# Transposing the q and k stacks of three attention branches on TensorE instead of by DMA

## The chip, the cores and the metric

The kernel runs on one core of a Trainium2 chip. The metric is the device time of one execution in microseconds (us). The engines are TensorE (PE in the profile, with PEld for its weight loads), VectorE (DVE), ScalarE (ACT), GpSimd (POOL) and SyncE (SP), which here only issues DMAs. Each engine takes its instructions from a queue of its own, in order. On-chip data lies in SBUF, the results of matmuls in PSUM; GpSimd does not read PSUM here.

## What is computed

One layer of a hybrid decoder over a sequence of 2048 positions with 1024 channels: an RMS norm, one input projection, three token mixers side by side, a SiLU gate on each, one output projection and the residual. Cut to what matters here:

```python
h = rms_norm(x, norm_g)
proj = einsum('bsd,de->bse', h, w_in)
# A) forgetting attention, 8 heads of 64: logits q.k/8 + c[t] - c[s], causal softmax, times v
fq = rms_norm(heads(fq), q_norm_g); fk = rms_norm(heads(fk), k_norm_g)
fox = forgetting_attention(fq, fk, fv, log_f) * silu(fg)
# B) trailing means over 2/4/8/16 positions, a linear map for each group
pool = multiscale_pool(px, w_pool, pool_scale) * silu(pg)
# C) stick-breaking attention, 4 heads of 64: sigmoids with running products, strictly causal
sb = stick_breaking_attention(sq, sk, sv) * silu(sg)
out = x + einsum('bse,ed->bsd', concat([fox, pool, sb]), w_out)
```

## The kernel before

The sequence is cut into 16 blocks of 128 positions and runs backwards. A value that needs more than 16-bit precision is carried as a pair of f16 numbers, a high part and a low part (`pairs16`, L339: ScalarE casts the high part, VectorE subtracts it from the source to get the low part). So a projection is three f16 matmuls for each of 8 slices of the 1024 channels (`project`, L315).

The work comes in five phases: `a` and `b` (four forgetting heads each, class `Fox`), `s` (four stick-breaking heads, class `Stick`, with the pooling branch `p` woven in) and `o` (the output projection). In `a`, `b` and `s` each of the 16 blocks does the following.

- Project q, k, v and the gate into PSUM (`proj`, tiles `pqk` and `pvg`). In `a` and `b`, `stages` (L704) then normalises q and k through ScalarE, VectorE and GpSimd into the SBUF tile `qn`; in `s`, q and k are taken straight from PSUM.
- `stacks` (L455) builds the f16 pairs of q and k in the tile `st` (high and low part of k, high and low part of q, each of 4 heads and 64 channels wide) and issues one DMA transpose on SP's queue into `qT` (L464). A function `place` is put off by `SCD` = 5 steps: on VectorE it copies the transposed k into the key cache `Kc` (L467), and then, by two copies of 64 partitions each, writes q's low and high parts in swapped order over the place where k stood (L469). After that the first half of `qT` holds q with its parts swapped, the second half q in order.
- `qk` computes the scores of a head in one or two chunks of at most 1024 columns. `scores` (L396) takes one of the two PSUM tiles with the tag `sp` and does two matmuls for each 512 columns (L404), one with each half of `qT`, so that all four products of the parts come together. In `a` and `b` VectorE adds the forget bias and takes the maximum (L736), and ScalarE does the exponentials (L746). In `s` ScalarE does sigmoids (L875), GpSimd masks them (L877, L878), and VectorE scans the products (L883).
- `split_t` (L416) makes an f16 pair of each chunk in a buffer `pp` (ScalarE or VectorE casts, L430 and L432; GpSimd subtracts, L433) and transposes it by DMA from SP's queue (L435). The `pp` buffers are a ring of `PB` = 5, which the rows of x also use (`transpose_rows`, L371) before their DMA transpose.
- `pv` multiplies by v, three heads later (`DEPTH` = 3, L1202). In `s`, `steps` (L814) also makes differences of v on PE (L821) from a pair that has just been cast.

What sets the order: `projections` (L1120) is a generator that yields after every slice of a projection, that is after three matmuls; `advance` (L1190) pulls it and calls `tick` at each step, which runs what `later` put off. The main loop (L1218) lays the heads of block k between the steps by a written list of due steps (`LEADS`, L76). This gives the program order. The order in each engine's queue is then made from it at compile time by the framework's scheduler (L1309), which takes program order as priority and its own model for durations.

Of the kernel before, what the change touches and what calls it, by code (L numbers as in the profile page):

```python
# [10 lines left out]
F16 = mybir.dt.float16  # L11
BF16 = mybir.dt.bfloat16
AF = mybir.ActivationFunctionType
ALU = mybir.AluOpType
# [4 lines left out]
P = 128  # L19
KT = 8  # L20
D = 1024
HD = 64
NH = 4
# [13 lines left out]
GR4 = 0  # L37
GR2 = 1
QSB = 2
SWE = 'vv'  # L40
KCE = 'v'
SCD = 5
M5 = 2
FE = 's'
OMS = 'g'
# [17 lines left out]
LEAD = 10  # L63
DEPTH = 3
TB = 4
PB = 5
FHIA = 'sv'
FHIB = 'ssv'
FLO = 'gg'
# [56 lines left out]
def hybrid(ctx: ExitStack, tc, xN, w_in, w_pT, w_out, ng, b_f, qg, kg, w_pool, p_scale, bands, out):  # L126
    nc = tc.nc
    v, s, g, t, sy = nc.vector, nc.scalar, nc.gpsimd, nc.tensor, nc.sync
# [4 lines left out]
    const = ctx.enter_context(tc.tile_pool(name="const", bufs=1))  # L133
# [3 lines left out]
    at = ctx.enter_context(tc.tile_pool(name="at", bufs=2))  # L137
    sm = ctx.enter_context(tc.tile_pool(name="sm", bufs=3))
    pj = ctx.enter_context(tc.tile_pool(name="pj", bufs=PJ, space=PSUM))
    ps = ctx.enter_context(tc.tile_pool(name="ps", bufs=2, space=PSUM))  # L140
# [5 lines left out]
    def pick(pattern, k):  # L146
        return {"v": v, "g": g, "s": s}[pattern[k % len(pattern)]]
# [6 lines left out]
    def later(k, fn):  # L154

        if k:
            waiting.append([k, fn])
        else:
            fn()
# [19 lines left out]
    ident = const.tile([P, P], F32, name="ident")  # L179
# [4 lines left out]
    g.affine_select(tri, ones, [[-1, P]], ALU.is_ge, 0.0, base=0, channel_multiplier=1)  # L184
    id16 = const.tile([P, P], BF16, name="id16")
    g.tensor_copy(id16, ident)
    zero = at.tile([P, P], BF16, name="zero", tag="oa")
    g.memset(zero, 0.0)
    cmask = const.tile([P, P], BF16, name="cmask")
# [37 lines left out]
    class Weights:  # L227
# [12 lines left out]
        def measure(self, kt):  # L240
            for a, n in enumerate(self.widths):
                wr = self.raw(kt, a, "wm")
                junk = at.tile([P, n], BF16, name=f"jk{self.name}_{kt}_{a}", tag="pp", bufs=PB)
                acc = self.fa[:, a * KT + kt:a * KT + kt + 1]
# [53 lines left out]
        def weigh(self, kt, eng):  # L298
            held = self.held[:, kt]
            junk = at.tile([P, self.widths[0]], BF16, name=f"jh_{kt}", tag="L", bufs=LB) if eng is s else at.tile([P, self.widths[0]], BF16, name=f"jh_{kt}", tag="pp", bufs=PB)  # L300
            acc = self.fa[:, kt:kt + 1]
# [37 lines left out]
    def pairs16(hi, lo, src, scale, eng=v):  # L339

        s.activation(hi, src, AF.Copy, scale=scale)
        eng.scalar_tensor_tensor(lo, src, scale, hi, ALU.mult, ALU.subtract)  # L342
# [6 lines left out]
    def squares(j, xn):  # L349
        junk = at.tile([P, D], BF16, name=f"xj{j}", tag="pp", bufs=PB)  # L350
        ssq = sm.tile([P, 1], F32, name=f"ssq{j}", tag="ssq")
        s.activation(junk, xn, AF.Square, accum_out=ssq)
        return ssq
# [17 lines left out]
    def transpose_rows(src, scale, tag, park=None):  # L371
        pp = at.tile([P, 2 * D], F16, name=f"pp{tag}", tag="pp", bufs=PB)
        pairs16(pp[:, 0:D], pp[:, D:2 * D], src, scale[:, 0:1], pick(XLO, park or 0))
        x = xp.tile([P, 2, KT, P], F16, name=f"xT{tag}", tag="xT", bufs=XB)
        sy.dma_start_transpose(x.rearrange("p a k t -> p (a k) t"), pp)
        if park is not None:
            keep_x(park, x)
        return x
# [37 lines left out]
    def split_t(p32, n, tag, h, all_, hi_eng, lo_eng):  # L416
# [3 lines left out]
        if k == 0:  # L420
            shared["pp"] = at.tile([P, 2 * CH], F16, name=f"pp{tag}", tag="pp", bufs=PB)
            shared["tt"] = at.tile([P, 2 * CH // P, P], F16, name=f"tt{tag}", tag="tt", bufs=TB)
# [27 lines left out]
    def heads(ap):  # L450
        return ap.rearrange("p (h d) -> p h d", h=NH)
# [2 lines left out]

    def stacks(tag, j, qsrc, ksrc, sc, Kc):  # L455

        st = at.tile([P, 2, NH, P], F16, name=f"st{tag}", tag="qs", bufs=QSB)
        pairs16(st[:, 0, :, 0:HD], st[:, 0, :, HD:P], heads(ksrc), sc)
        pairs16(st[:, 1, :, 0:HD], st[:, 1, :, HD:P], heads(qsrc), sc)
        qT = at.tile([P, 2 * NH, P], F16, name=f"qT{tag}", tag="qT", bufs=QTB)  # L460
        if j % 4 == 3:
            Kc[j // 4] = big.tile([P, NH, 512], F16, name=f"K{tag}", tag="K", bufs=KB)
        o_ = (j % 4) * P
        sy.dma_start_transpose(qT, st.rearrange("p a h d -> p (a h d)"))  # L464

        def place():
            pick(KCE, 0).tensor_copy(Kc[j // 4][:, :, o_:o_ + P], qT[:, 0:NH])  # L467
            for k in range(2):
                pick(SWE, k).tensor_copy(qT[k * HD:k * HD + HD, 0:NH], qT[HD - k * HD:P - k * HD, NH:2 * NH])  # L469
            placed.add(tag)  # L470

        later(SCD, place)
        return qT
# [839 lines left out]
```

## Time and profile before

| | us |
|---|---|
| median of 3 runs | 1418.04 |
| lowest and highest run | 1412.04, 1418.87 |
| profiled execution, its own time | 1417.73 |
| its span, first to last instruction | 1415.7 |

| engine | busy, us | share of the span | instructions |
|---|---|---|---|
| PE | 1209.6 | 85% | 9068 |
| DVE | 997.1 | 70% | 2093 |
| ACT | 702.0 | 50% | 1356 |
| POOL | 634.1 | 45% | 615 |

All of these come from one profiled execution. A matmul's busy time includes its way through the array, which overlaps with the next matmul, so a busy PE is not a PE at its peak. [...] "L467" is line 467 of the kernel. Where a row says that an engine waited for something, the engine's queue had nothing else to run in that time: the waiting instruction was at its head.

### The profile page before, as it was taken

The numbers are of one execution on the slowest core, as the hardware profiler recorded it, in microseconds if no ns is written. First come the engines' busy times: TensorE is split into PE (matmuls) and PEld (weight loads), VectorE is DVE, ScalarE is ACT, GpSimd is POOL, SyncE is SP. The second block draws the span as 40 slices with busy tenths as digits, with TensorE's granted clock in tenths as the row PEclk, the third lists the DMA queues.
The fourth block names the chain that finished last, engine by engine and source line by source line (L and its number), as shares of the span: only waits on it lengthen the run. The fifth ranks groups of instructions, "written<-read, shape, count | busy, mean of one in ns | idle before, by whom it ended". The sixth has DMA issues, their size and how long they took to land.

```text
span 1415.7 us, 24981 instructions
## 1 busy us (share of the span) xinstructions
PE 1209.6 (85%) x9068; PEld 642.2 (45%) x9068; DVE 997.1 (70%) x2093; ACT 702.0 (50%) x1356; POOL 634.1 (45%) x615
## 2 busy tenths in 40 slices
PE   7788879787887889897987888978988997779998
PEld 3344445444444445454544544444544553444443
DVE  5777889889998567786888655556574669865731
ACT  6555546555554446664667644545455564432210
POOL 0133345445455234553656654555455464623300
PEclk9889899999998989999999999999999999989999
DMA  6689999998999999996999998687886888999853
GB/s 215 176 169 203 214 188 221 200 196 182 210 210 209 210 227 207 202 177 135 184 217 191 227 207 186 146 158 161 173 175 142 172 196 226 225 277 287 225 160 89
DMA packets 617068, 275.25 MB, mean 194 GB/s; under 512 B 552561, under 2 KB 590833, under 8 KB 616945
## 3 DMA queue, kind: packets, MB, share of 16 engines
q1 hardware_dynamic: 605600, 239.93, 80.4%
q10 hardware_dynamic: 10832, 33.67, 7.9%
q8 instruction: 71, 1.16, 0.4%
q14 instruction: 53, 0.43, 0.1%
q0 software_dynamic: 512, 0.07, 0.0%
HBM read 102.60 MB, written 34.67 MB: 97 GB/s over the span
## 4 chain that ended last, share of the span: by engine, by line
PE 18%; DVE 11%; issue 9%; DMA 8%; POOL 8%; ACT 5%; SPq 1%; POOLq 0%; ACTq 0%; DVEq 0%
PE pr L319 11%; DVE rrs L883 5%; POOL pps L433 5%; DMA qTs<-sts 2%; DMA qTb<-stb 2%; PE pqks L319 2%; DVE Lb L736 2%; DMA xTm<-ppm 1%; ACT pps L430 1%; ACT Lb L746 1%; POOL rrs L877 1%; PE sps L404 1%; DMA ttb<-ppb 1%; PE pp L319 1%; POOL ppb L433 1%
## 5 line engine op out<-in xcount | busy, mean ns | idle before, releaser
L433 POOL TENSOR_TENSOR ppb<-Lb,ppb 128x1024 f16<-128x1024 f32 (+7 forms) x96 | 151.6, 1593 | 150.3 <-ACT ppb L430 68.9
L433 POOL TENSOR_TENSOR ppa<-La,ppa 128x1024 f16<-128x1024 f32 (+7 forms) x96 | 152.7, 1604 | 141.9 <-DVE ppa L432 53.4
L433 POOL TENSOR_TENSOR pps<-rrs,pps 128x640 f16<-128x640 f32 (+7 forms) x96 | 171.3, 1790 | 75.2 <-ACT pps L430 74.8
L319 PE MATMUL pr<-wo,xTm 128*128 128x512 f16 x768 | 172.2, 386 | 8.1 <-DMA xTm<-ppm 5.3
L883 DVE TENSOR_TENSOR_SCAN rrs<-rrs 128x640 f32<-128x640 f32 (+7 forms) x64 | 109.5, 1714 | 68.3 <-POOL rrs L877 43.8
L430 ACT CAST pps<-rrs 128x640 f16<-128x640 f32 (+7 forms) x96 | 76.1, 796 | 142.0 <-DVE rrs L883 127.3
L746 ACT ACTIVATE Lb<-Lb,nmb 128x640 f32<-128x640 f32 (+7 forms) x96 | 85.6, 892 | 80.3 <-DVE nmb L740 75.4
L746 ACT ACTIVATE La<-La,nma 128x640 f32<-128x640 f32 (+7 forms) x96 | 85.5, 891 | 77.0 <-DVE nma L740 53.5
L319 PEld LDWEIGHTS <-xTm 128*128 128x128 f16 x768 | 75.8, 99 | 100.9 <-issue 8.8
L319 PEld LDWEIGHTS <-xTb 128*128 128x128 f16 x768 | 77.0, 103 | 92.6 <-issue 16.7
L404 PE MATMUL spa<-Ka,qTa 128*128 128x512 f16 (+3 forms) x320 | 83.7, 371 | 36.8 <-DVE mma L736 35.2
L319 PEld LDWEIGHTS <-xTs 128*128 128x128 f16 x768 | 74.4, 99 | 86.9 <-issue 3.3
L319 PEld LDWEIGHTS <-xTx 128*128 128x128 f16 x720 | 72.6, 105 | 89.3 <-issue 25.5
L319 PE MATMUL pqkb<-wb,xTb 128*128 128x512 f16 x384 | 101.7, 408 | 0.3 <-ACT wb L277 0.3
L404 PE MATMUL spb<-Kb,qTb 128*128 128x512 f16 (+3 forms) x320 | 79.7, 361 | 23.4 <-DVE mmb L736 20.7
L319 PE MATMUL pp<-auxp,xTp 128*128 128x512 f16 x384 | 96.9, 404 | 0.0
L319 PE MATMUL pqka<-wa,xTx 128*128 128x512 f16 x336 | 95.3, 434 | 1.3 <-DVE cr L562 1.3
L319 PE MATMUL pvgb<-wb,xTb 128*128 128x512 f16 x384 | 96.1, 390 | 0.0
L875 ACT ACTIVATE rrs<-sps,nc 128x640 f32<-128x640 f32 (+7 forms) x96 | 80.5, 863 | 30.3 <-PE sps L404 28.8
L319 PE MATMUL pqks<-ws,xTs 128*128 128x512 f16 x384 | 92.1, 385 | 0.7 <-DVE vo L342 0.4
L404 PE MATMUL sps<-Ks,qTs 128*128 128x512 f16 (+3 forms) x320 | 73.2, 361 | 21.2 <-DVE qTs L469 16.6
L319 PE MATMUL pvgs<-ws,xTs 128*128 128x512 f16 x384 | 90.9, 379 | 0.0
(307 smaller groups left out, 2804.4 us busy)
## 6 DMA issues: line engine op xcount, KB each, us to landing
xn<-in_xN_dram SPq DMA_DIRECT2D x16, 512.0 KB, 5.5
xTd<-xTx ACTq DMA_DIRECT2D x16, 512.0 KB, 4.3
xTb<-xTd ACTq DMA_DIRECT2D x16, 512.0 KB, 4.6
xTs<-xTd ACTq DMA_DIRECT2D x16, 512.0 KB, 4.3
xTp<-xTd ACTq DMA_DIRECT2D x16, 512.0 KB, 4.3
go<-gat SPq DMA_DIRECT2D x16, 512.0 KB, 7.6
mt<-mix SPq DMA_DIRECT2D x16, 512.0 KB, 5.6
xr<-in_xN_dram SPq DMA_DIRECT2D x16, 512.0 KB, 4.4
```

What stands on the lines that cost most here:

```text
L319: t.matmul(psum, x[:, xa, kt, :], wt[:, wa, c0:c0 + n], start=(kt == 0 and i == 0), stop=(kt == KT - 1 and i == 2))
L404: t.matmul(sp[:, b - c0 + off:e - c0 + off], qT[:, a * NH + h, :], Kc[b // 512][:, h, b % 512:b % 512 + e - b], start=(a == 0), stop=(a == ...
L430: s.copy(hi, p32)
L433: lo_eng.tensor_tensor(lo, p32, hi, ALU.subtract)
L736: v.tensor_tensor_reduce(lt, sp, negc[:, h, c0:c1_], c1[:, 0:1], 4 * NEG if a == 0 else mm[:, a - 1:a], ALU.add, ALU.max, mm[:, a:a + 1])
L746: s.activation(ls[a], ls[a], AF.Exp, bias=nm[:, 0:1], accum_out=la[:, a, h:h + 1])
L875: s.activation(gg, sp, AF.Sigmoid, scale=self.nc2[:, 0:1])
L877: g.affine_select(gg[:, 0:P], gg[:, 0:P], [[1, P]], ALU.is_gt, 1.0, base=0, channel_multiplier=-1)
L883: v.tensor_tensor_scan(gg, gg, gg, init, ALU.mult, ALU.bypass)
```

## The change

The stack gets a third plane, so that q's high part and q's low part each stand twice, side by side, in planes of their own. The DMA transpose goes. `place` takes a score tile (`sp`) from PSUM, transposes the 4 blocks of k and the 8 of q on PE with an f16 identity, and copies the results by ScalarE straight into the key cache and into `qT`. With q's parts written twice, the two matmuls of a score are k with the doubled high part and k with the doubled low part; the four products are the same as before. `place` comes 2 steps after the stack instead of 5. The ring of part buffers has 4 buffers instead of 5.

```diff
-SWE = 'vv'
-KCE = 'v'
-SCD = 5
+SCD = 2
...
-PB = 5
+PB = 4
...
+    idh = const.tile([P, P], F16, name="idh")
+    g.tensor_copy(idh, ident)
...
     def stacks(tag, j, qsrc, ksrc, sc, Kc):
 
-        st = at.tile([P, 2, NH, P], F16, name=f"st{tag}", tag="qs", bufs=QSB)
+        st = at.tile([P, 3, NH, P], F16, name=f"st{tag}", tag="qs", bufs=QSB)
         pairs16(st[:, 0, :, 0:HD], st[:, 0, :, HD:P], heads(ksrc), sc)
-        pairs16(st[:, 1, :, 0:HD], st[:, 1, :, HD:P], heads(qsrc), sc)
+        hi, lo = (st[:, a].rearrange("p h (r d) -> p h r d", r=2) for a in (1, 2))
+        s.activation(hi, heads(qsrc).unsqueeze(2).broadcast_to([P, NH, 2, HD]), AF.Copy, scale=sc)
+        for r in range(2):
+            v.scalar_tensor_tensor(lo[:, :, r], heads(qsrc), sc, hi[:, :, r], ALU.mult, ALU.subtract)
         qT = at.tile([P, 2 * NH, P], F16, name=f"qT{tag}", tag="qT", bufs=QTB)
         if j % 4 == 3:
             Kc[j // 4] = big.tile([P, NH, 512], F16, name=f"K{tag}", tag="K", bufs=KB)
         o_ = (j % 4) * P
-        sy.dma_start_transpose(qT, st.rearrange("p a h d -> p (a h d)"))
 
         def place():
-            pick(KCE, 0).tensor_copy(Kc[j // 4][:, :, o_:o_ + P], qT[:, 0:NH])
-            for k in range(2):
-                pick(SWE, k).tensor_copy(qT[k * HD:k * HD + HD, 0:NH], qT[HD - k * HD:P - k * HD, NH:2 * NH])
+            pt = ps.tile([P, 2048], F16, name=f"pt{tag}", tag="sp")
+            for h in range(NH):
+                t.transpose(pt[:, 1024 + h * P:1024 + (h + 1) * P], st[:, 0, h, :], idh)
+            for a in range(2):
+                for h in range(NH):
+                    b = (a * NH + h) * P
+                    t.transpose(pt[:, b:b + P], st[:, 1 + a, h, :], idh)
+            s.copy(Kc[j // 4][:, :, o_:o_ + P], pt[:, 1024:1536].rearrange("p (h b) -> p h b", h=NH))
+            s.copy(qT, pt[:, 0:1024].rearrange("p (h b) -> p h b", h=2 * NH))
             placed.add(tag)
 
         later(SCD, place)
```

## Rows read from the trace of the kernel before

**Rows 1.** Table of stretches, a, b and s: us, then busy us of each engine.

```profile
60.00:400.00 340.00, 281.50 (x2101) 151.52 (x2102) 285.99 (x794) 188.30 (x431) 153.42 (x126) 0.90 0.96 197
400.00:755.00 355.00, 302.13 (x2261) 165.48 (x2259) 269.28 (x630) 193.22 (x419) 171.88 (x133) 0.94 0.95 197
755.00:1180.00 425.00, 367.72 (x3163) 199.30 (x3164) 264.06 (x351) 229.75 (x371) 235.19 (x302) 0.95 0.86 181
```

**Rows 2.** The page's chain that ended last, by engine and by line.

```profile
PE 18%; DVE 11%; issue 9%; DMA 8%; POOL 8%; ACT 5%; SPq 1%; POOLq 0%; ACTq 0%; DVEq 0%
PE pr L319 11%; DVE rrs L883 5%; POOL pps L433 5%; DMA qTs<-sts 2%; DMA qTb<-stb 2%; PE pqks L319 2%; DVE Lb L736 2%; DMA xTm<-ppm 1%; ACT pps L430 1%; ACT Lb L746 1%; POOL rrs L877 1%; PE sps L404 1%; DMA ttb<-ppb 1%; PE pp L319 1%; POOL ppb L433 1%
```

**Rows 3.** Waits of DVE: us in total, times, longest us.

```profile
DVE Ks L467 <- DMA qTs<-sts: 35.5, 12, 5.4
...
DVE Kb L467 <- DMA qTb<-stb: 23.5, 12, 5.9
...
DVE Ka L467 <- DMA qTa<-sta: 13.9, 8, 3.0
```

**Rows 4.** Timeline of 925 to 942 us: start, us, instruction, [idle before, releaser].

```profile
929.57 1.70 SPq L464 DMA_TRANSPOSE qTs<-sts  x1
...
934.96 0.29 DVE L467 COPY Ks<-qTs 128x512 f16<-128x512 f16 x1 [4.46 <-DMA qTs<-sts]
...
935.93 2.10 PE L404 MATMUL sps<-Ks,qTs 128*128 128x128 f16 x6 [7.12 <-DVE qTs L469]
```

**Rows 5.** Stretches as in rows 1; the third number from the end is the granted clock.

```profile
928.00:936.00 8.00, 0.88 (x5) 0.27 (x4) 3.46 (x6) 2.33 (x3) 2.62 (x5) 0.74 0.96 215
936.00:940.00 4.00, 4.00 (x32) 2.24 (x33) 3.09 (x3) 2.67 (x4) 1.21 (x4) 0.67 0.35 68
```

**Rows 6.** Waits of PE.

```profile
PE spa L404 <- DVE mma L736: 35.2, 20, 4.9
PE spb L404 <- DVE mmb L736: 20.7, 13, 4.1
...
PE pd L821 <- ACT vr L341: 18.5, 5, 7.8
PE sps L404 <- DVE qTs L469: 16.6, 5, 7.1
```

**Rows 7.** Whole run, DVE busy on L467, then on L469.

```profile
0.00:1415.00 1415.00, 26.30 (x48) 0.94 0.89 195
...
0.00:1415.00 1415.00, 51.07 (x96) 0.94 0.89 195
```

**Rows 8.** Tile sts, casts and low parts: duration in ns, min/median/max.

```profile
L341 ACT ACTIVATE sts<-pqks x32: 359/378/387, 750.0 to 1169.6; 128x256 f16<-128x256 f32 x32
L342 DVE SCALAR_TENSOR_TENSOR sts<-pqks,sts x32: 397/416/425, 752.0 to 1171.0; 128x256 f16<-128x256 f32 x32
```

**Rows 9.** Tile sts, the DMA transposes: issue in ns, landing in us.

```profile
L464 SPq DMA_TRANSPOSE qTs<-sts x16: 1232/1554/3673, 756.6 to 1173.0; - x16
...
DMA to landing us min/median/max: 3.2/3.7/5.7
```

**Rows 10.** Waits of SP's queue.

```profile
SPq L435 <- POOL ppb L433: 65.2, 33, 5.1
```

**Rows 11.** Timeline of PE, 517.8 to 518.2 us.

```profile
517.87 0.22 PE L446 MATMUL ob<-Vb,ttb 128*128 128x128 f16 x1
517.92 0.19 PE L447 MATMUL ob<-Vb,ttb 128*128 128x64 f16 x1
517.95 0.22 PE L446 MATMUL ob<-Vb,ttb 128*128 128x128 f16 x1
```

**Rows 12.** Groups of ACT by shape: busy us, mean ns, idle before.

```profile
L707 ACT ACTIVATE qnb<-pqkb 128x512 f32<-128x512 f32 x16 | 9.4, 586 | 11.4 <-PE pqkb L319 8.0 <-DVE stb L342 3.4
...
L430 ACT CAST pps<-rrs 128x1024 f16<-128x1024 f32 x28 | 29.2, 1044 | 55.0 <-DVE rrs L883 43.7 <-DMA tts<-pps 6.3 <-DVE mx L1038 5.0
```

**Rows 13.** Waits of ACT.

```profile
ACT pps L430 <- DMA tts<-pps: 7.7, 3, 6.0
...
ACT sta L341 <- DMA xTx<-ppx: 4.6, 2, 3.4
```

## Prediction

> **What bounds it now.** I read the table of stages first, because the share of busy time means little over stages with different limits. The profile splits into a (60 to 400 us), b (400 to 755), s (755 to 1180) and the output projection; the 48 calls of `stacks`, 16 a stage, lie in the first three. There TensorE (PE) is busy 83 to 87%, VectorE (DVE) 84, 76 and 62%, ScalarE (ACT) 54 to 55% [rows 1]. So PE is nearest to full, but no engine is. The chain that ended last says the same: PE 18% of the span, DVE 11%, DMA 8%, ACT 5%, out of some 60% that it covers, and two of its DMA steps are this change's, qTs and qTb, 2% each [rows 2]. A kernel like this is held by waits in queues that run in order, so next I ask which waits hang on the step that goes.
>
> DVE stands still 72.9 us (35.5 + 23.5 + 13.9, 32 of the 48 calls) with `place`'s first copy at the head of its queue until the DMA transpose has landed [rows 3]. What is behind it is delayed though it needs no q or k: in s these are the scans of the stick-breaking products. One such wait shows the path: the transpose is issued at 929.57, the copies start at 934.96, the scores at 935.93, 6.4 us later, and PE has stood for 7.1 us [rows 4]. [...] PE waits 16.6 us directly for these copies in s, and 55.9 us in a and b for DVE to read a score bank (35.2 + 20.7) [rows 6].
>
> **Taken away.** (1) The wait of DVE. In s I count 0.8 of 35.5, that is 28 us: the scans stand right behind it, and 6.4 us become about 2.7 (12 x 0.053 on PE, 1.63 on ACT, both from rows below, and some 0.4 for three hand-overs, an estimate). In a and b I count half of 37.4, 19 us: DVE is fuller there and catches up less, but other work fills part of each wait. Ends: 0 and 73. (2) 144 DVE copies, 26.3 + 51.1 = 77.4 us [rows 7]; against them one more low part of q each call, 48 x 0.416 = 20 [rows 8]. Of the net 57 I count a quarter, 14 us, a little over DVE's share of the chain (11 of 60), since it is busiest in a. Ends: 0 and 57. (3) PE's five waits in s for the copies: the clock falls less; 5 x 1.3 = 6 us. The 16.6 us themselves lie in (1). (4) 48 issues in SP's queue, 1.55 us each at the median in s, and transfers of 3.2 to 5.7 us [rows 9]. I count nothing: SP's other transposes wait for GpSimd to finish a part, 65.2 us for b's alone [rows 10], and PV runs three heads behind. If that cover is thin it is a gain, at most the 1% of the chain that is a transpose for PV, 14 us [rows 2]. POOL's queue loses nothing and gains one copy of the identity, in the opening, off the path.
>
> **Added.** (5) 576 transposes on PE. The trace has no f16 transpose. The nearest rows are PV's matmuls of 128 and 64 f16 columns, which start every 80 ns as a pair [rows 11]: 192 columns in 80 ns, so 53 ns for 128 columns and 30.5 us in all (61 at half clock). The 0.22 us beside each is its latency, which overlaps. PE has 13 to 17% idle, so half lies in idle time: 15 us. Ends: 0 and 61. (6) ACT: two copies from PSUM, 512 columns at 0.59 and 1024 at 1.04, and q's high cast at 512 columns in place of 256, 0.59 against 0.38 [rows 8, 12], the nearest rows (those of 512 columns read PSUM, that of 1024 SBUF): 48 x 1.84 = 88 us. ACT then is at about 60%; its share of the chain is 5 of 60, so 8 us. Behind these copies in ACT's queue are the exponentials and sigmoids, whose readers are DVE and GpSimd. Ends: 0 and 88. (7) A new wait: PE's transposes need the stack, and behind them stand projections, scores and PV. The nearest row is `steps`, where PE takes the two parts of v straight from ACT and DVE: 18.5 us for 16 blocks [rows 6], 1.16 us a block, 55 us over 48 calls. That matmul follows its casts at once in the program, the transposes only two projection steps later, so I take 10. Ends: 0 and 55. (8) `place` takes one of the two score banks: 55.9 us of waits fell on 192 score tiles of a and b, 0.29 each, and 48 x 0.29 = 14; the freed DVE returns part, so 8. Ends: 0 and 28, for a bank held twice as long. (9) One part buffer less. With five, ACT shows waits for a transpose out of that ring of 7.7 us (parts of s) and 4.6 (rows of x) [rows 13]. I take 4; ends 0 and 25, twice their sum. Earlier placing (two steps for five) costs nothing by itself; it is what (7) bounds.
>
> Sum: 28 + 19 + 14 + 6 = 67 gained, 15 + 8 + 10 + 8 + 4 = 45 lost, 22 us net. The profiled execution took 1417.73 us (span 1415.7 and 2.0 around it), 0.3 under the median of 1418.04, so **1396 us**.
>
> [...]
>
> **Rivals.** Measuring this kernel can tell about 0.5% (7 us) from no change.
> - *The waits count in full*, 0.16. For it: in the sample PE stands too while DVE waits, and the clock falls [rows 4, 5]. Terms (1) to (3) are then 73 + 14 + 6, less 45: 1370.
> - *Hidden anyway*, 0.15. DVE catches up, a third of the waits counts: 24 + 14 + 6 against 45, 1419. For it: DVE has 16 to 38% idle in these stages. Against: scans follow the wait directly in s.
> - *PE waits in place of DVE* (slower), 0.13. The transposes stand in PE's queue and the stack comes late from ACT and DVE, at the rate of `steps`: term (7) is 55 and the kernel takes 1441. It decides from 32 us on, 0.67 us a call. For it: PE has the least idle time, and everything queues behind it. Against: two projection steps of slack.
> - *The clock falls around each transpose group* (slower), 0.09. Each fall costs 1.3 us as in [rows 5]; if all 48 groups bring one, 62 us, 1458; if half do, 1427; from 17 groups on there is no gain. For it: a group comes with a wait for the stack ahead and two copies behind. Against: projections stand on both sides, and a group is 0.64 us of a block's 21 to 27. [...]
>
> That the change does not do what it says has little room: the transpose's input and output are written out. But each engine's order is made anew at compile time, so waits elsewhere may move by chance; that is in the width.
>
> **Numbers.** My own case has 0.47 and runs from 1383 to 1410. Faster: 0.47 + 0.16 = 0.63. Same: 0.15. Slower: 0.13 + 0.09 = 0.22. The range reaches down to the full count, 1370, and up to 1434, between half and all of the slower cases, which leaves about 2 in 10 outside.
>
> **What would show it.** DVE: no idle time for q and k, 57 us less busy. ACT: 88 us more busy, the two copies near 0.6 and 1.04. PE: 576 more matmuls starting 53 ns apart, with waits for `st` of about 10 us in all. The scans of s should show less idle time around them, and no transposes of `st` on SP. PE waits for `st` of over 32 us, a granted clock below 0.937, or waits for score banks clearly over 70 us would make the forecast wrong; so would a DVE whose idle time only moved to scores, banks or parts.

## The result, and the profile after

| | before | after |
|---|---|---|
| median, us | 1418.45 | 1487.73 |
| lowest and highest run, us | 1412.04, 1420.55 | 1484.19, 1490.35 |
| profiled execution, its own time and its span, us | 1417.73, 1415.7 | 1489.36, 1487.7 |

The kernel before has one run more here than in the table ahead of the prediction. The kernel became slower: the ratio is 1.0495 with a 95% interval of 1.0453 to 1.0536. The time lies far outside the predicted range. The busy times of the kernel after:

```profile
PE 1246.7 (84%) x9644; PEld 682.3 (46%) x9644; DVE 935.8 (63%) x1997; ACT 783.1 (53%) x1451; POOL 642.8 (43%) x616
```

The work changed as forecast: PE has 576 instructions more, DVE is 61 us less busy (935.8 against 997.1), ACT 81 us more (783.1 against 702.0). The span grew by 72 us all the same, so the work alone does not account for it. The table of stages says where to look (columns as in [rows 1]; the borders are moved to where the stages now lie):

```profile
60.00:440.00 380.00, 286.88 (x2214) 159.27 (x2214) 259.13 (x757) 208.63 (x455) 155.02 (x122) 0.87 0.76 167
440.00:825.00 385.00, 322.34 (x2494) 184.87 (x2492) 257.53 (x607) 229.30 (x460) 179.50 (x135) 0.92 0.83 171
825.00:1250.00 425.00, 376.44 (x3370) 211.26 (x3370) 246.93 (x323) 254.20 (x404) 231.82 (x302) 0.96 0.81 169
```

In stage a PE is busy 75% of the stretch and DVE 68%, where it was 83% and 84%; the DMA share fell from 0.96 to 0.76 and PE's granted clock, a share of its full speed, from 0.90 to 0.87. GpSimd went from 45% to 41%, and ACT stayed at 55% though it has more to do. So no engine became the bound: PE, DVE, GpSimd and the DMA engines all got idler at once. Stage s has no such drop in PE, 89% against 87%. To size this I looked at one tile of each stage, the transposed q, and at its score matmuls: how many, their durations in ns, the start of the first and of the last in us. First the kernel before, then the kernel after:

```profile
L404 PE MATMUL spa<-Ka,qTa x320: 216/379/634, 54.4 to 435.8; 128*128 128x512 f16 x112, 128*128 128x128 f16 x16, 128*128 128x256 f16 x16, 128*128 128x384 f16 x16
...
L404 PE MATMUL spb<-Kb,qTb x320: 216/379/634, 440.9 to 790.0; 128*128 128x512 f16 x112, 128*128 128x128 f16 x16, 128*128 128x256 f16 x16, 128*128 128x384 f16 x16
...
L404 PE MATMUL sps<-Ks,qTs x320: 216/379/634, 796.1 to 1236.2; 128*128 128x512 f16 x112, 128*128 128x128 f16 x16, 128*128 128x256 f16 x16, 128*128 128x384 f16 x16
```

```profile
L404 PE MATMUL spa<-Ka,qTa x320: 216/379/634, 63.7 to 487.6; 128*128 128x512 f16 x112, 128*128 128x128 f16 x16, 128*128 128x256 f16 x16, 128*128 128x384 f16 x16
...
L404 PE MATMUL spb<-Kb,qTb x320: 219/379/634, 491.8 to 865.3; 128*128 128x512 f16 x112, 128*128 128x128 f16 x16, 128*128 128x256 f16 x16, 128*128 128x384 f16 x16
...
L404 PE MATMUL sps<-Ks,qTs x320: 216/379/634, 868.5 to 1309.2; 128*128 128x512 f16 x112, 128*128 128x128 f16 x16, 128*128 128x256 f16 x16, 128*128 128x384 f16 x16
```

The first score comes 9.3 us later (63.7 against 54.4). The last of a is 51.8 us later (487.6 against 435.8), so a lost 42.5 us more. The last of b is 75.3 us later, another 23.5. The last of s is 73.0 us later, 2.3 us regained, and what follows is 1 us shorter. So the loss is the opening, a and b, and nothing in s, where the largest gain had been expected.

Which wait grew there? Waits of DVE in the kernel after (us in total, times, longest):

```profile
DVE rrs L892 <- POOL rrs L886: 66.8, 36, 6.0
DVE Lb L745 <- PE spb L404: 40.7, 23, 9.0
...
DVE La L745 <- PE spa L404: 19.6, 16, 4.4
...
DVE Lb L745 <- PE spb L406: 13.3, 6, 4.4
```

The waits of [rows 3] are gone, all of them. In their place DVE waits for scores: 40.7 + 19.6 + 13.3, with a small fourth row (2.2) 75.8 us in all. In the kernel before these four rows add up to 11.1. And the scan of s waits 66.8 us for the mask of GpSimd, where it waited 43.8. The same waits in the kernel before, without its two small rows of 1.2 us each:

```profile
DVE rrs L883 <- POOL rrs L877: 43.8, 28, 4.1
...
DVE Lb L736 <- PE spb L404: 5.5, 8, 1.0
...
DVE La L736 <- PE spa L404: 3.2, 3, 2.1
```

Waits of PE in the kernel after:

```profile
PE pf L328 <- DMA xTx<-ppx: 28.3, 6, 8.3
PE spa L404 <- DVE mma L745: 21.5, 22, 6.4
...
PE pts L472 <- DVE sts L342: 16.7, 5, 6.6
PE pta L472 <- DVE sta L342: 10.4, 3, 5.4
PE ptb L472 <- DVE stb L342: 8.2, 4, 2.9
PE spb L404 <- DVE mmb L745: 6.9, 10, 1.1
```

Against [rows 6], PE waits less for DVE to read a score (21.5 + 6.9 against 55.9), since DVE is now the one that has to wait, and it waits 35.3 us for the stack at the transposes (16.7 + 10.4 + 8.2). The rows so far say that scores come late, 65 us more of waiting at DVE, and not what holds them; the 35.3 us are about half of the loss. PE also waits more for DMA transposes that the change does not touch, those of the rows of x ahead of a projection and of the parts ahead of PV in a and b: 28.3 us for x as shown, 32.2 and 19.8 for the parts of b and a, 80.3 in all. In the kernel before it is 42.3 (11.0 + 20.6 + 10.7), of which x has:

```profile
PE pf L328 <- DMA xTx<-ppx: 11.0, 7, 2.8
```

The order of events tells what holds the scores. Here is the timeline of the kernel after (start, us, instruction), from which I took the score matmuls, the last read of a score, PE's longest wait and the stack's steps between 125 and 158 us:

```profile
125.02 1.01 ACT L478 COPY qTa<-pta 128x1024 f16<-128x1024 f16 x1
...
126.91 0.59 PE L404 MATMUL spa<-Ka,qTa 128*128 128x512 f16 x2
...
133.79 0.88 DVE L745 CUSTOM_DVE_ANT_0 La<-spa,negca,c 128x640 f32<-128x640 f32 x1 [0.25 <-POOL ppa L433]
...
137.13 0.19 PE L328 MATMUL pf<-wa,xTx 128*128 128x16 f16 x1 [8.30 <-DMA xTx<-ppx]
...
154.03 0.41 DVE L342 SCALAR_TENSOR_TENSOR sta<-qna,sta 128x256 f16<-128x256 f32 x1
...
157.00 0.39 PE L472 MATMUL pta<-idh,sta 128*128 128x128 f16 x4
157.22 0.61 PE L476 MATMUL pta<-idh,sta 128*128 128x128 f16 x8
...
157.67 0.38 PE L404 MATMUL spa<-Ka,qTa 128*128 128x256 f16 x2
...
157.87 0.58 ACT L477 COPY Ka<-pta 128x512 f16<-128x512 f16 x1 [2.10 <-PE pta L476]
```

The scores that start at 157.67 belong to a block whose q and k were ready at 126.03: they start before the copies of 157.87, so they cannot need the stack that was just transposed. The last read of a score tile ended at 134.67, so from then on both score tiles were empty. Still no score ran until 157.67, 23 us later and 30 us after the last one, and then they came at once behind the transposes of the next block's stack, even before the copies had released that tile; the first of them therefore used the other one. What held them is then not a full tile but a turn. This is the theory that the experiments below test: the score tiles are handed out in program order, `place` now takes one, and when the order of PE's queue is made at compile time, the scores written behind `place` stay behind its transposes. The next block's stack was ready at 154.4 and its transposes ran at 157.00 without a wait, so in this stretch the stack itself cost PE nothing.

In the same stretch PE had too little else to run. Table of stretches of the kernel after:

```profile
127.00:157.00 30.00, 20.88 (x156) 10.59 (x154) 17.78 (x61) 14.91 (x35) 11.39 (x9) 0.83 0.84 182
...
157.00:167.00 10.00, 10.00 (x83) 6.15 (x81) 5.29 (x17) 6.64 (x13) 3.46 (x3) 1.00 0.59 176
```

PE is busy 21 of 30 us and then without a gap. Of the 9 us in which it stood, 8.3 were spent at the head of the next block's projection, waiting for the DMA transpose of its rows of x (137.13 above). From 134.67 on, scores that were ready could have filled the rest of that wait, but they stood behind it in PE's queue. Scores come in bursts: first DVE and ACT have nothing, then PE has everything at once. I counted the pauses of over 8 us between one score matmul and the next in the timeline of PE. Before there were 6 in a and 3 in b (59 and 26 us together), and none ended behind a transpose. After there are 11 and 8 (207 and 107 us), and all 19 end right behind a group of transposes. In s there were 16 (190 us) and are 14 (169 us).

The added work itself costs what it was priced at. The tile `pta` of the kernel after, durations in ns (min/median/max), first and last start:

```profile
L476 PE MATMUL pta<-idh,sta x128: 219/219/314, 51.4 to 444.6; 128*128 128x128 f16 x128
...
L477 ACT COPY Ka<-pta x16: 566/585/597, 52.6 to 444.9; 128x512 f16<-128x512 f16 x16
L478 ACT COPY qTa<-pta x16: 1002/1018/1047, 53.0 to 445.3; 128x1024 f16<-128x1024 f16 x16
```

A group of 8 takes 0.61 us (157.22 above) and one of them 0.219, so they start every (0.61 - 0.219) / 7 = 0.056 us, at a granted clock of 1.00 in that stretch.

### The profile page after: what moved, and what is told of

It is laid out like the page before. It is cut to its first block, busy times and chain, and to the rows that moved or that the text cites. A ratio compares the mean times of both kernels' runs of the same rounds, so it can differ in the third digit from the quotient of the medians.

```text
span 1487.7 us, 26006 instructions
## 1 busy us (share of the span) xinstructions
PE 1246.7 (84%) x9644; PEld 682.3 (46%) x9644; DVE 935.8 (63%) x1997; ACT 783.1 (53%) x1451; POOL 642.8 (43%) x616
## 4 chain that ended last, share of the span: by engine, by line
PE 33%; DVE 16%; DMA 14%; issue 10%; ACT 8%; POOL 8%; SPq 2%; ACTq 0%; POOLq 0%; DVEq 0%
PE pr L319 11%; DVE rrs L892 4%; POOL pps L433 4%; DMA tta<-ppa 3%; PE pqkb L319 3%; DMA ttb<-ppb 3%; PE pqka L319 3%; DMA tts<-pps 2%; DVE La L745 2%; PE pvgb L319 2%; DVE Lb L745 2%; PE spa L404 1%; PE pqks L319 1%; PE spb L404 1%; PE pvgs L319 1%
## 5 line engine op out<-in xcount | busy, mean ns | idle before, releaser
L433 POOL TENSOR_TENSOR ppa<-La,ppa 128x1024 f16<-128x1024 f32 (+7 forms) x96 | 161.1, 1687 | 138.7 <-DVE ppa L432 51.8
L433 POOL TENSOR_TENSOR ppb<-Lb,ppb 128x1024 f16<-128x1024 f32 (+7 forms) x96 | 154.6, 1627 | 150.3 <-ACT ppb L430 55.7
L433 POOL TENSOR_TENSOR pps<-rrs,pps 128x640 f16<-128x640 f32 (+7 forms) x96 | 178.6, 1865 | 89.5 <-ACT pps L430 89.1
L892 DVE TENSOR_TENSOR_SCAN rrs<-rrs 128x640 f32<-128x640 f32 (+7 forms) x64 | 109.5, 1712 | 93.4 <-POOL rrs L886 66.8
L319 PEld LDWEIGHTS <-xTb 128*128 128x128 f16 x768 | 73.6, 100 | 87.9 <-issue 12.3
L404 PE MATMUL spa<-Ka,qTa 128*128 128x512 f16 (+3 forms) x320 | 82.9, 374 | 30.1 <-DVE mma L745 21.5
L745 DVE CUSTOM_DVE_ANT_0 Lb<-spb,negcb,c 128x640 f32<-128x640 f32 (+7 forms) x64 | 60.4, 946 | 59.5 <-PE spb L404 38.2
L319 PE MATMUL pqkb<-wb,xTb 128*128 128x512 f16 x384 | 93.4, 387 | 4.5 <-ACT wb L277 2.1
L319 PE MATMUL pp<-auxp,xTp 128*128 128x512 f16 x384 | 93.4, 393 | 0.9 <-DVE vo L342 0.9
L319 PE MATMUL pqka<-wa,xTx 128*128 128x512 f16 x336 | 92.0, 426 | 0.0
L446 PE MATMUL ob<-Vb,ttb 128*128 128x128 f16 x544 | 63.2, 228 | 32.5 <-DMA ttb<-ppb 32.2
```

What stands on the lines that cost most here:

```text
L319: t.matmul(psum, x[:, xa, kt, :], wt[:, wa, c0:c0 + n], start=(kt == 0 and i == 0), stop=(kt == KT - 1 and i == 2))
L404: t.matmul(sp[:, b - c0 + off:e - c0 + off], qT[:, a * NH + h, :], Kc[b // 512][:, h, b % 512:b % 512 + e - b], start=(a == 0), stop=(a == ...
L433: lo_eng.tensor_tensor(lo, p32, hi, ALU.subtract)
L446: t.matmul(o[:, 0:P], tt[:, b, :], vt, start=first, stop=False)
L745: v.tensor_tensor_reduce(lt, sp, negc[:, h, c0:c1_], c1[:, 0:1], 4 * NEG if a == 0 else mm[:, a - 1:a], ALU.add, ALU.max, mm[:, a:a + 1])
L892: v.tensor_tensor_scan(gg, gg, gg, init, ALU.mult, ALU.bypass)
```

## Experiments

The theory at this point: the loss is the turn of the score tiles, which `place` takes too early, 2 steps behind the stack. The rivals: the ring of part buffers, 4 for 5; the added work on PE and ACT; the direct wait of PE for the stack; and chance, since any edit makes the order of the queues anew. A ratio is to the kernel before on the same chip, with its 95% interval.

**The ring of part buffers and the step of `place`.** Nine kernels change only these two numbers. In the kernel after, a fifth part buffer takes the room of the second stack buffer, so there `QSB` goes from 2 to 1 with it; a difference between ring 4 and ring 5 is that of both.

The kernel before with a ring of 4:

```diff
-PB = 5
+PB = 4
```

> The kernel before with one part buffer less (4 for 5) and nothing else. Ring theory (most of the 70 us is the lost part buffer, since in stages a and b of the changed kernel all engines got idler at once and chains run through the transposes of parts): 1460 to 1490. PE-wait theory (the changed kernel loses because PE stands for the stack and ACT stands for PE): 1415 to 1425. Order theory (any edit makes a new order of the queues, away from the written list of due steps, and costs some per cent by chance): anything from 1400 to 1470, with no one wait that grows.

The kernel after with a ring of 5:

```diff
-QSB = 2
+QSB = 1
...
-PB = 4
+PB = 5
```

> The changed kernel with 5 part buffers as before; room for it comes from one stack buffer instead of two, which is free again once PE has transposed it. Ring theory: the forecast's case without its ring term, 1390 to 1425. PE-wait theory: 1480 to 1490 as the change. Order theory: somewhere between, with waits scattered.

The kernel after with `place` at 5 steps:

```diff
-SCD = 2
+SCD = 5
```

> The changed kernel with place put off by 5 steps as before instead of 2. PE-wait theory: the waits of PE for the stack (50 us with those for other engines) mostly go, 1435 to 1455. Ring theory: 1480 to 1490. Order theory: 1450 to 1490.

The kernel before with `place` at 2 steps:

```diff
-SCD = 5
+SCD = 2
```

> The kernel before with place put off by 2 steps instead of 5. Ring theory: 1410 to 1435, the DVE copies stand somewhat earlier in DVE's queue and wait longer for the DMA transpose (73 us before, up to 110). PE-wait theory: the same. Order theory: 1430 to 1470, since the order is new.

The kernel after with both, a ring of 5 and 5 steps:

```diff
-QSB = 2
-SCD = 2
+QSB = 1
+SCD = 5
...
-PB = 4
+PB = 5
```

> The changed kernel with 5 part buffers (one stack buffer) and place put off by 5 steps, both as before. Additive: the ring gave 22 us and the steps 44, so 1488 - 66 = 1420. If the two overlap (both act through stage a): 1430 to 1445. If what is left is the transposes themselves (31 us of PE, 80 us of ACT), it stays at 1425 or more; if the release of DVE is worth what I forecast, 1395 to 1410.

The kernel after with a ring of 5 and 10 steps, which is the edit of the last with `SCD = 10`:

```diff
-SCD = 2
+SCD = 10
```

> As the run before, with place put off by 10 steps. Waiting theory (PE or the score banks wait for the stack): the waits of PE at the transposes fall from some 35 to under 10 us and the time by another 5 to 20 against place after 5. Order theory: no trend, within 15 us either way. In s the leads are as short as 8 steps, so waits for qT may come back there (up to 15 us).

The kernel before with 10 steps:

```diff
-SCD = 5
+SCD = 10
```

> The kernel before with place put off by 10 steps, so that the DMA transposes have landed when DVE comes to the copies: the price of the 73 us of DVE waits by itself, without PE transposes. My forecast's terms: 28 + 19 us, 1365 to 1380. If the waits are hidden in work that DVE catches up with: 1405 to 1420. In s it may wait for qT instead (up to 15 us).

The kernel after with 10 steps alone, its ring left at 4:

```diff
-SCD = 2
+SCD = 10
```

> The change with one number altered: place put off by 10 steps instead of 2, the ring at its 4 buffers. Bank theory (the loss is the score tile that place takes in its turn of the ring and holds until the stack is made): 1400 to 1420, the ring of 4 costing 5 to 15 us against 1399 with a ring of 5. Ring theory (the ring of 4 costs 22 us wherever place stands): 1418 to 1425.

The kernel after with a ring of 5 and 14 steps, again with `QSB = 1` and `PB = 5`:

```diff
-SCD = 2
+SCD = 14
```

> Ring of 5 and place after 14 steps instead of 10. If the time still falls with the step (1465, 1446, 1399 at 2, 5, 10): 1385 to 1395, with the rest of the pauses ahead of a transpose gone. If 10 steps are past the knee: 1395 to 1410, and in s, where leads are as short as 8 steps, scores wait for qT.

Measured, with two sums from the waits: DVE for scores (the rows of `La` and `Lb` at the bias, as above), and PE at a transpose for the stack (from DVE or ACT; for the change the 35.3 us above and two small rows).

| kernel | median, us | ratio | DVE for scores, us | PE for the stack, us |
|---|---|---|---|---|
| after, ring 4, step 2 (the change) | 1487.73 | 1.0495 [1.0453, 1.0536] | 75.8 | 38.0 |
| after, ring 4, step 5 | 1443.63 | 1.0201 [1.0159, 1.0243] | 50.0 | 27.0 |
| after, ring 4, step 10 | 1409.35 | 0.9967 [0.994, 0.9994] | 22.3 | 15.1 |
| after, ring 5, step 2 | 1465.25 | 1.0354 [1.0309, 1.0398] | 84.2 | 27.9 |
| after, ring 5, step 5 | 1446.05 | 1.0236 [1.0211, 1.0261] | 55.5 | 15.1 |
| after, ring 5, step 10 | 1399.09 | 0.9906 [0.9869, 0.9943] | 24.8 | 15.1 |
| after, ring 5, step 14 | 1413.78 | 1.0003 [0.9973, 1.0033] | 30.3 | 11.3 |
| before, ring 4, step 5 | 1424.38 | 1.006 [1.0019, 1.0101] | 5.5 | |
| before, ring 5, step 2 | 1422.18 | 1.0049 [1.003, 1.0069] | 8.4 | |
| before, ring 5, step 10 | 1413.51 | 1.0005 [0.9981, 1.003] | 8.5 | |

The step decides. From step 2 to step 10 the ratio falls by 5.3% with the ring of 4 and by 4.5% with that of 5, and with it DVE's wait for scores; the whole loss of the change goes with one number. The same number does next to nothing in the kernel before, where `place` takes no score tile: 0.5% at step 2, nothing at step 10. So a new order by itself, without a score tile, moved the time by 0.6% at most in these three edits of the kernel before. PE's direct wait for the stack is not what decides: with the ring of 5 it is 15.1 us at step 5 and at step 10, and the times are 47 us apart; at step 14 it is shortest, and the time is worse than at 10. PE's waits for the other DMA transposes, 80.3 us in the change, go with the step too: 58.4 us at step 5 and 33.1 at step 10, both with the ring of 4. How much of these waits scores in time would have covered was not tried.

The ring matters less: 1.4% at step 2, nothing at 5 (0.35% the other way), 0.6% at step 10, and 0.6%, 8.5 us, in the kernel before. Its wait is the same in both, that of ACT for a part buffer. First a row of the kernel before with a ring of 4, then one of the kernel after:

```profile
ACT pps L430 <- DMA tts<-pps: 39.9, 15, 7.1
```

```profile
ACT pps L430 <- DMA tts<-pps: 38.2, 15, 7.2
```

Before it was 7.7 [rows 13]: 32 us more waiting for 8.5 us of time.

The kernel before with 10 steps was meant to take DVE's waits for the DMA transposes away. It did not: they are 36.7 + 26.7 + 13.5 = 76.9 us, against 72.9 in [rows 3]. So it says nothing of what those waits are worth.

**A held score tile by itself, in the kernel before.** If the turn is the cause, a kernel that keeps its DMA transposes and takes a score tile for hardly any work must lose the time as well. Each block here gets one PE transpose and one copy of 8 columns, whose result nothing uses:

```diff
+    idh = const.tile([P, P], F16, name="idh")
+    g.tensor_copy(idh, ident)
...
+        def hold():
+            pt = ps.tile([P, 2048], F16, name=f"pt{tag}", tag="sp")
+            t.transpose(pt[:, 0:P], st[:, 1, NH - 1, :], idh)
+            hd = sm.tile([P, 8], F16, name=f"hd{tag}", tag="hd", bufs=1)
+            s.copy(hd, pt[:, 0:8])
+
+        later(2, hold)
         later(SCD, place)
```

> The kernel before, DMA transposes and all, with one small thing added to each stack: 2 steps later a score tile is taken, one of the 4 blocks of q is transposed into it on PE and 8 columns are copied out by ScalarE, for nothing. 48 transposes and 48 copies of 0.2 us, 12 us of work at most. Bank theory: 1440 to 1480, with DVE waiting for scores tens of us. Work theory (the 576 transposes and 80 us of copies are the loss): 1414 to 1425.

The same with 10 steps:

```diff
-        later(2, hold)
+        later(10, hold)
```

> As the run before with the tile taken 10 steps after the stack instead of 2; the work added is the same. Bank theory: 1414 to 1430, most of it the opening's 9 us. Work theory: the same time as with 2 steps.

Measured: 1484.08 us at 2 steps, ratio 1.0522 [1.0448, 1.0596], and 1437.43 at 10 steps, 1.0169 [1.012, 1.0219]. Of the one with 2 steps, the waits of PE for the stack, and the tile `pta` (columns as above):

```profile
PE pts L476 <- DVE sts L344: 18.5, 6, 5.9
...
PE pta L476 <- DVE sta L344: 11.2, 7, 4.1
```

```profile
L476 PE MATMUL pta<-idh,sta x16: 219/230/294, 50.4 to 415.3; 128*128 128x128 f16 x16
L478 ACT COPY hda<-pta x16: 141/165/165, 52.4 to 415.6; 128x8 f16<-128x8 f16 x16
```

48 transposes of 0.23 us and 48 copies of 0.165 us, 19 us of work in all and none of it large, cost 71 us, as much as the whole change. DVE's waits for scores are 40.0 us, against 11.1 before, and 19.8 with 10 steps. Of its 21 pauses of over 8 us in a and b, 18 end behind a transpose (before: none of 9). PE waits for the stack 18.5 us in s and 11.2 in a, as in the kernel after. The added work, the ring and the copies are thereby out as the main cause: none of them is in this kernel. Two things differ from the change. Stage s loses too, some 10 us (against the kernel before the last score of b comes 57.8 us later and that of s 68.0). And at 10 steps the hold still costs 24 us.

**The hold moved to other tiles.** In the kernel after, the transposed stack goes to two of the projections' PSUM tiles:

```diff
-            pt = ps.tile([P, 2048], F16, name=f"pt{tag}", tag="sp")
+            pk = pj.tile([P, 1024], F16, name=f"pk{tag}", tag="pj")
             for h in range(NH):
-                t.transpose(pt[:, 1024 + h * P:1024 + (h + 1) * P], st[:, 0, h, :], idh)
+                t.transpose(pk[:, h * P:(h + 1) * P], st[:, 0, h, :], idh)
+            pt = pj.tile([P, 1024], F16, name=f"pt{tag}", tag="pj")
...
-            s.copy(Kc[j // 4][:, :, o_:o_ + P], pt[:, 1024:1536].rearrange("p (h b) -> p h b", h=NH))
+            s.copy(Kc[j // 4][:, :, o_:o_ + P], pk[:, 0:512].rearrange("p (h b) -> p h b", h=NH))
```

> The changed kernel (4 part buffers, place after 2 steps) with the transposes written into two of the four projection banks instead of one of the two score tiles. Bank theory (scores that come after the transposes in the ring of two cannot start before the stack is made, transposed and copied, which is long in a and b and short in s): the first score of a comes 9 us earlier again, DVE's waits for scores (76 us against 11 before) fall to under 30, 1435 to 1460. Queue theory (the transposes block PE's queue itself): 1475 to 1495, and PE's waits for the stack stay at 50 us.

Measured: 1518.24 us, 1.075 [1.071, 1.0789]. This is worse than the change. Its waits of DVE for scores, then its waits of PE for the stack:

```profile
DVE Lb L746 <- PE spb L404: 9.1, 14, 2.0
```

```profile
PE pka L472 <- DVE sta L342: 40.3, 8, 15.9
...
PE pkb L472 <- DVE stb L342: 19.8, 7, 7.7
...
PE pks L472 <- DVE sts L342: 12.6, 5, 5.1
```

Neither range was met. The waits for scores are gone, 75.8 to under 10 us, and of its pauses in a and b only 2 of 26 end behind a transpose. So scores stand behind the transposes just where both take turns at the same tiles. But now the projections stand behind them, and PE waits 72.7 us for the stack, once for 15.9 us. ACT, too, now waits 44.1 and 28.7 us for part buffers of b and a (1.5 and 5.3 in the change). Which of these makes this kernel slower than the change was not tried. The first score came at 53.6 us.

**The opening.** The first two stacks go to projection tiles, in the kernel with a ring of 5 and step 10:

```diff
-            pt = ps.tile([P, 2048], F16, name=f"pt{tag}", tag="sp")
+            early = tag in ("a_0", "a_1")
+            if early:
+                pk = pj.tile([P, 1024], F16, name=f"pk{tag}", tag="pj")
+                pt = pj.tile([P, 1024], F16, name=f"pt{tag}", tag="pj")
+            else:
+                pt = ps.tile([P, 2048], F16, name=f"pt{tag}", tag="sp")
+                pk = pt[:, 1024:2048]
```

> Ring of 5 and place after 10 steps, and the transposes of the first two blocks of a in projection banks, since the score tiles hold the first two blocks' projections in the opening. Bank theory: the first score of a at 54 us instead of 63 us, as in the kernel before, and the whole 5 to 9 us shorter than 1399: 1388 to 1395. Otherwise 1397 to 1402.

Measured: 1413.93 us, 1.0001 [0.9973, 1.003], against 0.9906 without it. The first score came at 54.3 us in place of 63.4, as intended: in the opening both score tiles hold the projections of the first two blocks, and the stack takes its turn behind them. But the last score of a came at 445.8, against 444.2 without the edit, so the 9 us were gone again by the end of the stage. These starts are of single executions, and the one with the edit took 1403.73 us, 10 under its median. Neither range was met, and why the whole became slower is not known.

**What the removed and added parts are worth by themselves.** First the wait of DVE: in the kernel before, the three copies behind the DMA transpose go to ACT, so DVE has neither its waits nor its copies, and no score tile is taken:

```diff
-            pick(KCE, 0).tensor_copy(Kc[j // 4][:, :, o_:o_ + P], qT[:, 0:NH])
+            s.copy(Kc[j // 4][:, :, o_:o_ + P], qT[:, 0:NH])
             for k in range(2):
-                pick(SWE, k).tensor_copy(qT[k * HD:k * HD + HD, 0:NH], qT[HD - k * HD:P - k * HD, NH:2 * NH])
+                s.copy(qT[k * HD:k * HD + HD, 0:NH], qT[HD - k * HD:P - k * HD, NH:2 * NH])
```

> The kernel before with the three copies after the DMA transpose on ScalarE instead of VectorE: DVE no longer waits for the transpose (73 us) and does 77 us less; ACT takes some 48 x (0.6 + 2 x 0.6) = 85 us and waits in DVE's place. If DVE's waits are worth what I forecast (47 us, and 14 for its work): 1365 to 1385, with up to 20 given back by ACT. If they are mostly hidden: 1405 to 1425.

Measured: 1404.15 us, 0.993 [0.9902, 0.9957], 8 us faster. The waits of ACT, then of DVE in that kernel:

```profile
ACT Kb L467 <- DMA qTb<-stb: 34.1, 11, 8.2
ACT Ks L467 <- DMA qTs<-sts: 29.3, 10, 5.8
...
ACT Ka L467 <- DMA qTa<-sta: 20.3, 10, 4.8
```

```profile
DVE rrs L883 <- POOL rrs L877: 77.6, 40, 5.2
```

ACT now stands 83.7 us where DVE had stood 72.9, and on top of that DVE is 91 us less busy (906.2 against 997.1). The scan of s, which was to gain, waits 77.6 us for the mask in place of 43.8: the wait at the head of DVE's queue was followed by another that had been hidden behind it. The test is not pure, since ACT pays for the copies and waits; it shows that taking both from DVE at this price brings 8 us, far below the 61 us that were forecast for them.

Second the transposes: in the kernel after with a ring of 5 and step 10, every transpose is done twice into the same place:

```diff
-            for h in range(NH):
-                t.transpose(pt[:, 1024 + h * P:1024 + (h + 1) * P], st[:, 0, h, :], idh)
-            for a in range(2):
+            for _ in range(2):
                 for h in range(NH):
-                    b = (a * NH + h) * P
-                    t.transpose(pt[:, b:b + P], st[:, 1 + a, h, :], idh)
+                    t.transpose(pt[:, 1024 + h * P:1024 + (h + 1) * P], st[:, 0, h, :], idh)
+                for a in range(2):
+                    for h in range(NH):
+                        b = (a * NH + h) * P
+                        t.transpose(pt[:, b:b + P], st[:, 1 + a, h, :], idh)
```

> Ring of 5, place after 10 steps, and each of the 12 transposes done twice into the same place: 576 more on PE, 31 us at 53 ns, nothing else. My forecast's term (half shows): 1399 + 15 = 1410 to 1420. If PE's idle time takes them up: 1395 to 1405. If PE sets the pace: 1425 to 1435.

Measured: 1414.67 us, 1.0025 [0.9998, 1.0052]. PE is busy 1246.8 us against 1215.3, 31.5 more for 576 more. Against 0.9906 that is 1.2%, some 17 us, about half of the added work. The size is not settled: edits that add no work, the opening's and step 14, moved the time by 13 to 15 us.

Third the engine of the copies: in the same kernel the two copies out of PSUM go to DVE.

```diff
-            s.copy(Kc[j // 4][:, :, o_:o_ + P], pt[:, 1024:1536].rearrange("p (h b) -> p h b", h=NH))
-            s.copy(qT, pt[:, 0:1024].rearrange("p (h b) -> p h b", h=2 * NH))
+            v.tensor_copy(Kc[j // 4][:, :, o_:o_ + P], pt[:, 1024:1536].rearrange("p (h b) -> p h b", h=NH))
+            v.tensor_copy(qT, pt[:, 0:1024].rearrange("p (h b) -> p h b", h=2 * NH))
```

> Ring of 5, place after 10 steps, with the two copies out of PSUM on VectorE instead of ScalarE: ACT has 48 x 1.6 = 77 us less, DVE as much or more. If ACT's load is what the change costs: below 1399, 1380 to 1392. If DVE's relief is what it brings: 1410 to 1430, back to the kernel before or worse.

Measured: 1397.84 us, 0.99 [0.988, 0.992], the same as with ACT. The page of this kernel:

```profile
PE 1218.1 (87%) x9644; PEld 669.4 (48%) x9644; DVE 979.1 (70%) x2093; ACT 711.2 (51%) x1355; POOL 637.3 (46%) x616
```

ACT has 69 us less to do (711.2 against 780.0) and DVE 33 more, and nothing changes. The only versions of the change that beat the kernel before by about 1% are these two with a ring of 5 and step 10; the copies on ACT in the kernel before gave 0.7%. For the kernel with ACT's copies, the waits of DVE that had grown in the kernel after:

```profile
DVE Lb L745 <- PE spb L404: 15.1, 19, 2.2
```

40.7 us became 15.1, and of 6 pauses of over 8 us left in a and b (77 us), 3 end behind a transpose.

## Why the prediction was wrong, step by step

**The failed step is term (8), with the sentence that earlier placing costs nothing by itself.** I saw that `place` takes one of two score tiles, and priced it as a tile held twice as long, 8 us with ends of 0 and 28. That prices the tile from the moment when the transposes run. The tile is taken from its turn in program order, and that turn came 2 steps behind the stack's instructions. The scores behind it could not start before the next block's projection had run and its stack had gone through ACT, DVE and GpSimd, and in the stretch shown they waited with both tiles empty. Holding a tile with hardly any work in it costs 71 us at step 2 and 24 at step 10 (the kernel before with a hold). In the kernel after, the step alone is worth 75 us: its ratio falls from 1.0495 to 0.9967, which is 0.0528 x 1418. In s, q and k come straight from PSUM and the stack has no such way to go; in the change s lost nothing. That is a net figure: s also lost its waits of [rows 3], and with the hold alone, which keeps them, it lost some 10 us. That the length of the stack's way is the reason that a and b lose more was read from the timelines, not tried by itself.

**Terms (1) and (2), DVE's waits and work**, 61 us counted as gained. The waits went and the work went, as said. But taking both away by other means gave 8 us, with ACT paying for it. What was too large is at least the count of 0.8 in s: where the wait for q and k is gone, the scan waits longer for GpSimd's mask (43.8 us before, 66.8 after, 77.6 in that experiment). I had named what is behind the wait, but not what would be late next. How the 61 us divide between the two terms is not known.

**Term (3), the clock.** That each of PE's five waits for the copies costs 1.3 us was my estimate, and no run shows it. The trace of the kernel before shows one such fall: behind the wait of [rows 4] the granted clock was 0.50 of full speed from 936.00 to 938.50 us and 1.00 from 938.75 to 940.00, and 4 us at 0.67 [rows 5] lack 4 x 0.33 = 1.3 us. The mean granted clock of the profiled execution fell from 0.937 to 0.928 in place of rising: it was 0.83 in the 30 us shown, with PE busy 21 of them, and 1.00 in the next 10. The kernel before with a hold at step 2 is as low, 0.923, with 48 transposes in place of 576 and about as many pauses of over 8 us in a and b, 21 against 19 (9 in the kernel before, at 0.937): the fall came there with the pauses rather than with the number of transposes. The clock also weighs more than the 6 us that I gave it. At step 10 with the ring of 4 it is 0.951, and the busy times are:

```profile
PE 1218.2 (86%) x9644; PEld 668.6 (47%) x9644; DVE 940.4 (67%) x1997; ACT 775.7 (55%) x1451; POOL 633.1 (45%) x616
```

PE is busy 28.5 us less than in the change (1246.7) for as many instructions, about what the two clocks give (1246.7 x 0.928 / 0.951 = 1216.6). How much of that lies on the path is not shown.

**Term (4)** was zero and nothing contradicts it; it was not tried by itself.

**Terms (5) and (6), the added work.** The durations held: 56 ns against 53, 0.585 and 1.018 us against 0.59 and 1.04, ACT 81 us more busy against 88. The count of 15 us is near the 17 us for the transposes once more, which is within the scatter between orders. The 8 us for ACT were not measured by themselves: moving the copies from ACT to DVE changed nothing (1397.84 against 1399.09 us), which says only that they cost about as much on either engine.

**Term (7), PE at the stack**, was 10 with ends of 0 and 55; the rows show 35.3, above the 32 from which the rival was to decide. In s its 16.7 us replace 16.6 us of the same wait in [rows 6], so what is new is some 19 us. It has the same cause as (8), and it fell with the step.

**Term (9), the ring**, was 4 with ends of 0 and 25. Alone it measured 8.5 us in the kernel before.

**The rivals.** The slower one, PE waiting in place of DVE, had the direction and part of the mechanism, at 0.13, and its price was too low by 47 us because it counted only PE's direct wait. The clock rival, a fall with each transpose group, is not seen: with all transposes doubled the mean granted clock of the profiled execution was 0.958, against 0.955 with them once. The transposes stand in short groups between other matmuls, 8 in 0.61 us in the kernel after.

**What remains of the idea.** With the ring of 5 and step 10 the change gains 0.9%, 14.7 us, against 22 forecast; this rests on two runs, and on four with the copies on DVE. With the ring of 4 the gain is 0.3%. Some of the turn's price may be left in both, since a hold at 10 steps cost 24 us. Of the signs named ahead, three came: PE's waits for the stack over 32 us, a granted clock below 0.937, and a DVE whose idle time only moved to scores. The waits of PE for score tiles did not rise but fell; what the turn costs shows on DVE, whose waits for scores rose by 65 us.

**Open.** Kernels whose work is nearly the same (ring 5 at step 10, at step 14, with the opening's edit) lie 10 to 15 us apart, and why was not found; it limits what can be said of the transposes' cost. Runs of one kernel can scatter as much: those of step 14 lie between 1403.68 and 1419.74 us. Four kernels were slower than every range written down for them: the hold at 2 steps (by 4 us), the stack in projection tiles, the opening's edit and step 14; the hold at 10 steps was 7 us over what the theory of the turn gave it. So that theory has the direction and most of the size, and what adds to it is not known. Whether a shorter way to the stack would allow an early step was not tried.

## What to carry to other kernels

When a step that was a DMA moves to PE in a kernel scheduled like this one, it becomes a member of a ring of PSUM tiles: price it from its turn in program order until its release, not by its work, and place it where its input is ready, since what was behind it in the ring waited here even when the tiles were empty, 23 us in the stretch from 134.67 to 157.67. A sign of this is that the engines get idler together, the readers of one operation wait for it, and the engine that does it stands as well; then list the pauses of that operation and see what stands right ahead of each restart. The total of a wait is not its worth: ask what is late next behind it, here GpSimd's mask behind the DMA (43.8 us of waits before, 66.8 after).

## What the hardware showed that was not expected

The copies of the transposed stack out of PSUM were shorter on DVE than on ACT. The tile `pta` of the kernel that copies on DVE:

```profile
L477 DVE COPY Ka<-pta x16: 406/416/426, 54.8 to 412.6; 128x512 f16<-128x512 f16 x16
L478 DVE COPY qTa<-pta x16: 672/680/682, 55.2 to 412.9; 128x1024 f16<-128x1024 f16 x16
```

They take 416 and 680 ns where ACT takes 585 and 1018 for the same shapes. And in the kernel with every transpose done twice, 576 transposes more, in short groups between other matmuls, left the mean granted clock where it was (0.958 and 0.955).
